# VectorE takes the wide sums and products that GpSimd did in the mixers of a two-layer hybrid decoder

## The chip, the core and the metric

The kernel runs on one core of a Trainium2 chip. The metric is the device time of one execution, in microseconds (us). The times shown are the median of three runs; the profile is one further execution of the same program, with its own time. Engines are named as the profile names them: PE is TensorE (matmuls), DVE is VectorE (elementwise work), ACT is ScalarE (copies and functions), POOL is GpSimd, SP is SyncE, which here only issues DMAs.

## What is computed

Two decoder layers over 1024 positions of 1024 channels, all in float32. Each layer is a mixer and a squared-ReLU MLP of width 4096, each with a norm ahead of it and a norm behind it. Layer 0 mixes with a gated linear recurrence (HGRN2, 4 heads) and with retention (4 heads), layer 1 with a matrix memory (mLSTM, 4 heads).

```python
def reference(x, norm_g, ...):
    for l in range(DEPTH):                       # DEPTH = 2
        g = norm_g[l]
        h = rmsnorm(x, g[0])
        if l % 2 == 0:
            y = even_mixer(h, ev_w_in[e], lower_bounds[l], ev_hg_norm_g[e], ev_ret_norm_g[e], ev_w_out[e])
        else:
            y = odd_mixer(h, od_w_in[o], od_conv_w[o], od_conv_b[o], od_gate_b[o], od_ml_norm_g[o], od_w_out[o])
        x = x + rmsnorm(y, g[1])
        h = rmsnorm(x, g[2])
        x = x + rmsnorm(sq_relu_mlp(h, mlp_w1[l], mlp_w2[l]), g[3])
    return x
...
def sq_relu_mlp(h, w1, w2):
    return jnp.square(jax.nn.relu(h @ w1)) @ w2
```

The mixers are projections (`h @ w_in`), per-head work on chunks (gates, RoPE, scans over a state, a norm per head, a gate with silu or sigmoid) and an output projection (`y @ w_out`).

## The kernel before

**Matmuls.** Every large product is done in seven block products in place of eight (Strassen-Winograd), so both operands need sums and differences of blocks ahead of the matmuls. Every operand is also split in two parts of lower precision, hi and lo, and each product is three matmuls (hi·hi, hi·lo, lo·hi). A weight block therefore goes through these steps: a DMA lands it in one of four buffers `raw` (`pump`, line 140); the Winograd sums are made in place in `raw` and in one spare tile `ws` (`operands`, lines 174 to 207, the instruction itself on lines 188 and 190); ScalarE copies each operand to `hi` (line 160); VectorE subtracts to get `lo` (line 161). `hi` and `lo` have three buffers each, so up to three units are prepared ahead of TensorE.

**Who makes the sums.** `operands` takes an engine. The MLP (`mlp_plan`) passes VectorE; the mixers use the default, GpSimd (`pair_preps` and `group_preps`), so their sums run on line 190. Four more places in the mixers use GpSimd for wide operations: two of the four sums in `right_sums` (line 413, the activations' Winograd sums), the product in `silu_gate` (line 613), the last sum in `rope` (line 729), and the residual sum in `post_finish` (line 509), except in `mixer_last`, which passes VectorE. Besides, GpSimd does short chains of operations that are one column wide (1 element in each of 128 partitions): `rsq` (lines 127 and 128), lines 498, 516, 784, 786, 979, 980 and 982. Each head's scan squares a chunk on ScalarE, sends the sum of squares through such a chain on GpSimd and multiplies the output by the result on VectorE (lines 722, 788, 984). GpSimd also issues the DMAs that write the hidden activations of the MLP (line 1148).

**Order.** A planner sets the order of the instructions on each engine ahead of time, from its own estimate of the durations; each engine then runs its list in that order and waits where an operand is not there yet. Among the instructions that are ready, the planner takes the one that comes first in the program. `tc.high_priority(offset=-100)` moves the instructions in its block some 100 places back in that preference: in the kernel before, the split (lines 160 and 161) and VectorE's weight sums (line 188) are moved back in this way, GpSimd's weight sums (line 190) are not.

**Stages.** In the trace, layer 0's mixer takes about 0 to 680 us, its MLP 680 to 1500, layer 1's mixer 1500 to 2000, its MLP 2000 to 2704. Each mixer does its 1024 positions in two halves; between them lies the output projection with `post_finish` (`mixer_out`).

Of the kernel before, what the change touches and what calls it, by code (L numbers as in the profile page):

```python
# [7 lines left out]
F32 = mybir.dt.float32  # L8
# [4 lines left out]
ALU = mybir.AluOpType  # L13
# [56 lines left out]
def hybrid_kernel(ctx, tc, x, norm_g, pv_d, cs_d, mk_d, dec_d, cos_d, sin_d, wg_d, gb_d, w_ev, w_od, w_mlp, out):  # L70
    nc = tc.nc
# [5 lines left out]
    XT = ("z0", "z1", "x2", "x3")  # L77
# [78 lines left out]

    def split_w(dst, src):
        hi, lo = dst
        with tc.high_priority(offset=-100):
            nc.scalar.copy(out=hi, in_=src)  # L160
            nc.vector.tensor_tensor(out=lo, in0=src, in1=hi.bitcast(F32), op=ALU.subtract)  # L161

    def new_pair(i):
        return (wp.tile([P, 1024], F32R, tag="hi", name=f"whi{i}"),
# [6 lines left out]
        free_raw()  # L171
        return hl

    def operands(wide, eng):

        if wide:
            a11, a21, a22, a12 = (take_raw() for _ in range(4))
            t = wp.tile([P, 1024], F32, tag="ws", bufs=1, name="ws")
        else:
            r1, r2 = take_raw(), take_raw()  # L180
            a11, a12 = r1[:, 0:512], r1[:, 512:1024]
            a21, a22 = r2[:, 0:512], r2[:, 512:1024]
            t = wp.tile([P, 1024], F32, tag="ws", bufs=1, name="ws")[:, 0:512]

        def op(o, x0, x1, f):
            if eng is nc.vector:
                with tc.high_priority(offset=-100):
                    eng.tensor_tensor(out=o, in0=x0, in1=x1, op=f)  # L188
            else:
                eng.tensor_tensor(out=o, in0=x0, in1=x1, op=f)  # L190

        op(t, a21, a22, ALU.add)
        yield a11
        yield t
        op(a21, a11, a21, ALU.subtract)
        op(a11, t, a11, ALU.subtract)
        yield a11
        yield a12
        op(a12, a12, a11, ALU.subtract)
        if wide:  # L200
            free_raw()
        yield a21
        if wide:
            free_raw()
        yield a12
        yield a22
        free_raw(2)

    def rest_operands():

        r1, r2 = take_raw(), take_raw()
        a11, a12 = r1[:, 0:512], r1[:, 512:1024]
        a21, a22 = r2[:, 0:512], r2[:, 512:1024]
        t = wp.tile([P, 1024], F32, tag="ws", bufs=1, name="ws")[:, 0:512]

        def op(o, x0, x1, f):
            with tc.high_priority(offset=-100):
                nc.vector.tensor_tensor(out=o, in0=x0, in1=x1, op=f)

        op(t, a21, a22, ALU.add)  # L220
        op(a21, a11, a21, ALU.subtract)
        op(a11, t, a11, ALU.subtract)
        yield a11
        yield t
        yield a21
        op(a12, a12, a11, ALU.subtract)
        yield a12
        yield a22
        free_raw(2)

    def pair_preps(n, eng=nc.gpsimd, begun=0):
        gen = {}
        todo = [(p, o, o == 0, o == last) for p in range(n) for last in [4 if p < begun else 6] for o in range(last + 1)]

        def prep(j):
            def run(i):
                hl = new_pair(i)
                for e, (p, o, first, last) in enumerate(todo[2 * j:2 * j + 2]):
                    if first:
                        gen[p] = rest_operands() if p < begun else operands(False, eng)  # L240
                    c = slice(e * 512, (e + 1) * 512)
                    split_w((hl[0][:, c], hl[1][:, c]), next(gen[p]))
                    if last:
                        next(gen[p], None)
                return hl
            return run
        return [prep(j) for j in range((len(todo) + 1) // 2)]

    def group_preps(eng=nc.gpsimd):
        gen = []  # L250

        def prep(o):
            def run(i):
                hl = new_pair(i)
                if o == 0:
                    gen.append(operands(True, eng))
                split_w(hl, next(gen[0]))
                if o == 6:
                    next(gen[0], None)
                return hl  # L260
            return run
        return [prep(o) for o in range(7)]

    BEGUN = 3

    def mlp_plan():
        units = [std_prep] * BEGUN + pair_preps(16, nc.vector, BEGUN)
        for _ in range(7):
            units += group_preps(nc.vector)
        return units + [std_prep] * 8  # L270

    plan = []
# [48 lines left out]
    def add(o, x0, x1):  # L321
        nc.vector.tensor_tensor(out=o, in0=x0, in1=x1, op=ALU.add)  # L322
# [85 lines left out]

    def right_sums(stage):
        b11, b12, t1, t2, b21, t3, b22, t4 = (z[:, c] for z in stage for c in (L, R))  # L410
        for o, x0, x1, eng in ((t1, b12, b11, nc.vector), (t2, b22, t1, nc.vector),
                               (t3, b22, b12, nc.gpsimd), (t4, b21, t2, nc.gpsimd)):
            eng.tensor_tensor(out=o, in0=x0, in1=x1, op=ALU.subtract)  # L413

    def right_split(stage, k, p11, tiles):
        def split(dst, src):
# [76 lines left out]
        junk = sm.tile([P, 512], BF16, tag="junk", bufs=1, name="junk")  # L493
        nc.scalar.activation(out=junk, in_=y, func=AF.Square, accum_out=ss[t][:, n:n + 1])

    def post_finish(s, half, t, parts, ss, grow, tags=("z0", "z1"), eng=nc.gpsimd):
        tot = sm.tile([P, 1], F32, tag="tot", name=f"tot{s}_{half}_{t}")
        nc.gpsimd.tensor_tensor(out=tot, in0=ss[t][:, 0:1], in1=ss[t][:, 1:2], op=ALU.add)
        rs = sm.tile([P, 1], F32, tag="rs", name=f"rs{s}_{half}_{t}")
# [4 lines left out]
        for n in range(2):  # L504
            c = slice(n * 512, (n + 1) * 512)
            tmp = rg.tile([P, 512], F32, tag="tmp", bufs=2, name="ptmp")
            nc.vector.scalar_tensor_tensor(out=tmp, in0=parts[n], scalar=rs, in1=grow[:, c],
                                           op0=ALU.mult, op1=ALU.mult)
            eng.tensor_tensor(out=xt[:, c], in0=xt[:, c], in1=tmp, op=ALU.add)
            if s < 3:  # L510
                junk = sm.tile([P, 512], BF16, tag="junk", bufs=1, name="junk")
                nc.scalar.activation(out=junk, in_=xt[:, c], func=AF.Square, accum_out=s2[:, n:n + 1])
# [26 lines left out]
    def mixer_last(s, yT):  # L539

        grow = load_grow(s)
# [9 lines left out]
        xn = []  # L551
        for t in range(NT):
            post_sq(p1[t], t, 1, ss)
            xt = post_finish(s, 1, t, [y0[t], p1[t]], ss, grow, XT, nc.vector)
            parts = [kt.tile([P, HALF], F32, tag="kt", name=f"xk{s}_{t}_{n}") for n in range(2)]
            for n in range(2):
                nc.scalar.activation(out=parts[n], in_=xt[:, n * 512:(n + 1) * 512], func=AF.Copy, scale=rstd[1, t])
            xn.append(parts)
# [50 lines left out]
    def silu_gate(c, nm):  # L609
        for j in range(2):  # L610
            tmp = rg.tile([P, 2, 256], F32, tag="tmp", bufs=2, name=nm + f"sg{j}")
            nc.scalar.activation(out=tmp, in_=c[j], func=AF.Sigmoid)
            nc.gpsimd.tensor_tensor(out=c[j], in0=c[j], in1=tmp, op=ALU.mult)

    def scan_states(home, nm):

# [107 lines left out]
    def rope(c, cos, sin):  # L724
# [1 line left out]
        nc.vector.tensor_tensor(out=tmp[64:128], in0=c[0:64], in1=sin[0:64], op=ALU.mult)  # L726
        nc.vector.tensor_tensor(out=tmp[0:64], in0=c[64:128], in1=sin[64:128], op=ALU.mult)
        nc.vector.tensor_tensor(out=c, in0=c, in1=cos, op=ALU.mult)
        nc.gpsimd.tensor_tensor(out=c, in0=c, in1=tmp, op=ALU.add)

    def rt_keys(half, h, hT, cos, sin):
        nm = f"rt{half}_{h}"
# [691 lines left out]
```

## Time and profile before

| | before |
|---|---|
| median of 3 runs | 2698.22 us (2695.55 to 2700.66) |
| the profiled execution: its time | 2706.18 us |
| its span, from the first to the last instruction | 2704.4 us |
| PE busy | 2467.0 us (91%) |
| DVE busy | 1980.1 us (73%) |
| ACT busy | 1204.1 us (45%) |
| POOL busy | 780.4 us (29%) |

Busy time counts every stretch in which an engine has an instruction in work, once, however long that instruction takes; time in which the engine waits for a semaphore is idle, and the profile names what ended it.

### The profile page before, as it was taken

The numbers are of one execution on the slowest core, as the hardware profiler recorded it, in microseconds if no ns is written. First come the engines' busy times: TensorE is split into PE (matmuls) and PEld (weight loads), VectorE is DVE, ScalarE is ACT, GpSimd is POOL, SyncE is SP. The second block draws the span as 40 slices with busy tenths as digits, with TensorE's granted clock in tenths as the row PEclk, the third lists the DMA queues.
The fourth block names the chain that finished last, engine by engine and source line by source line (L and its number), as shares of the span: only waits on it lengthen the run. The fifth ranks groups of instructions, "written<-read, shape, count | busy, mean of one in ns | idle before, by whom it ended". The sixth has DMA issues, their size and how long they took to land. (4 is left out here: it accounts for less than half of the span.)

```text
span 2704.4 us, 41553 instructions
## 1 busy us (share of the span) xinstructions
PE 2467.0 (91%) x16432; PEld 2239.8 (83%) x16432; DVE 1980.1 (73%) x2574; ACT 1204.1 (45%) x2080; POOL 780.4 (29%) x895
## 2 busy tenths in 40 slices
PE   6989998898897999999998688988988999999997
PEld 6888888898885888899997588888866888899996
DVE  7898868889748666657774798789757666766774
ACT  5444454444445443443344544554455434443332
POOL 5665437665311111100001345376320111100000
PEclk8999999999998999999999899999999999999999
DMA  3222323122232434453453222232233433554353
GB/s 137 69 73 78 110 86 118 63 79 71 94 140 102 168 144 156 171 198 126 160 172 125 103 87 79 100 133 69 96 134 108 169 145 140 210 178 136 129 174 140
DMA packets 92836, 335.91 MB, mean 124 GB/s; under 512 B 10848, under 2 KB 10976, under 8 KB 92640
## 3 DMA queue, kind: packets, MB, share of 16 engines
q1 hardware_dynamic: 75744, 272.42, 29.6%
q0 software_dynamic: 16896, 60.83, 5.9%
q8 instruction: 129, 2.11, 0.3%
q14 instruction: 67, 0.55, 0.1%
HBM read 255.61 MB, written 77.59 MB: 123 GB/s over the span
## 5 line engine op out<-in xcount | busy, mean ns | idle before, releaser
L160 ACT CAST whi<-raw 128x512 fp32r<-128x512 f32 (+1 forms) x590 | 469.6, 812 | 684.4 <-PE p_0x L1168 72.4
L161 DVE TENSOR_TENSOR wlo<-raw,whi 128x512 fp32r<-128x512 f32 (+1 forms) x590 | 583.7, 1005 | 192.3 <-ACT whi L160 174.1
L1279 POOL TENSOR_TENSOR rs<-pm 128x1 f32<-128x1 f32 (+1 forms) x7 | 2.2, 321 | 635.2 <-ACT junk L1263 635.2
L190 POOL TENSOR_TENSOR raw<-raw,raw 128x1024 f32<-128x1024 f32 (+1 forms) x64 | 151.1, 2361 | 83.3 <-DVE wlo L161 41.5
L160 ACT CAST whi<-ws 128x512 fp32r<-128x512 f32 (+1 forms) x90 | 70.4, 782 | 101.4 <-POOL ws L190 34.7
L190 POOL TENSOR_TENSOR raw<-ws,raw 128x512 f32<-128x512 f32 (+1 forms) x44 | 88.6, 2014 | 62.1 <-DVE wlo L161 42.1
L161 DVE TENSOR_TENSOR wlo<-ws,whi 128x512 fp32r<-128x512 f32 (+1 forms) x90 | 96.8, 1075 | 9.0 <-ACT whi L160 9.0
L190 POOL TENSOR_TENSOR ws<-raw,raw 128x1024 f32<-128x1024 f32 x20 | 51.1, 2555 | 39.3 <-DMA raw<-in_w_ev_dram 30.8
L322 DVE TENSOR_TENSOR ya<-p_0x,ya 128x1024 f32<-128x1024 f32 x26 | 31.8, 1222 | 34.9 <-PE p_0x L1169 34.9
L188 DVE TENSOR_TENSOR raw<-raw,raw 128x1024 f32<-128x1024 f32 (+1 forms) x54 | 52.0, 963 | 0.5
L413 POOL TENSOR_TENSOR xb_a<-xb_a,xb_a 128x256 f32<-128x256 f32 x32 | 34.2, 1079 | 56.4 <-ACT xb_a L479 50.4
L190 POOL TENSOR_TENSOR ws<-raw 128x512 f32<-128x512 f32 x24 | 36.3, 1513 | 46.8 <-DMA raw<-in_w_od_dram 25.5
L190 POOL TENSOR_TENSOR raw<-raw 128x512 f32<-128x512 f32 x24 | 36.7, 1528 | 32.4 <-DVE wlo L161 32.4
L1166 PE MATMUL p_0v<-whi,h_5R1h 128*128 128x256 f32 x128 | 36.6, 286 | 3.1 <-ACT h_5R1h L1019 3.1
L1166 PE MATMUL p_0v<-whi,h_1R0h 128*128 128x256 f32 x128 | 35.9, 281 | 2.9 <-ACT m_15h L340 2.9
L1168 PE MATMUL p_0v<-whi,h_5R1l 128*128 128x256 f32 x128 | 36.7, 287 | 1.8 <-DVE h_5R1l L1020 1.8
L1166 PE MATMUL p_0x<-whi,h_4L1h 128*128 128x256 f32 x128 | 35.8, 280 | 1.1 <-ACT whi L160 1.1
L1166 PE MATMUL p_0x<-whi,h_2L0h 128*128 128x256 f32 x128 | 36.0, 281 | 0.6 <-ACT ya L1173 0.6
L1169 PE MATMUL p_0v<-wlo,h_5R1h 128*128 128x256 f32 x128 | 36.4, 285 | 0.0
L1168 PE MATMUL p_0z<-whi,h_3L4l 128*128 128x256 f32 x128 | 35.9, 280 | 0.3 <-DVE h_3L4l L1020 0.3
L1168 PE MATMUL p_0v<-whi,h_1R0l 128*128 128x256 f32 x128 | 35.8, 280 | 0.0
L1169 PE MATMUL p_0x<-wlo,h_2L0h 128*128 128x256 f32 x128 | 35.8, 279 | 0.0
(5385 smaller groups left out, 10111.4 us busy)
## 6 DMA issues: line engine op xcount, KB each, us to landing
raw<-in_w_mlp_dram SPq DMA_DIRECT2D x142, 512.0 KB, 3.7
h<-hid SPq DMA_DIRECT2D x112, 512.0 KB, 4.3
raw<-in_w_ev_dram SPq DMA_DIRECT2D x104, 512.0 KB, 3.3
raw<-in_w_od_dram SPq DMA_DIRECT2D x64, 512.0 KB, 3.3
xs<-xr SPq DMA_DIRECT2D x24, 512.0 KB, 2.9
xr<-xs SPq DMA_DIRECT2D x24, 512.0 KB, 5.2
xn<-in_x_dram SPq DMA_DIRECT2D x8, 512.0 KB, 3.8
xr<-in_x_dram SPq DMA_DIRECT2D x8, 512.0 KB, 5.3
```

Source lines behind the costliest of these rows:

```text
L160: nc.scalar.copy(out=hi, in_=src)
L161: nc.vector.tensor_tensor(out=lo, in0=src, in1=hi.bitcast(F32), op=ALU.subtract)
L188: eng.tensor_tensor(out=o, in0=x0, in1=x1, op=f)
L190: eng.tensor_tensor(out=o, in0=x0, in1=x1, op=f)
L322: nc.vector.tensor_tensor(out=o, in0=x0, in1=x1, op=ALU.add)
L413: eng.tensor_tensor(out=o, in0=x0, in1=x1, op=ALU.subtract)
L1166: nc.tensor.matmul(a, h[:, c], hi[:, w], start=first and k == 0 and t % 2 == 0, stop=False, skip_group_check=True)
L1168: nc.tensor.matmul(a, l[:, c], hi[:, w], start=False, stop=False, skip_group_check=True)
L1169: nc.tensor.matmul(a, h[:, c], lo[:, w], start=False, stop=k == 3, skip_group_check=True)
L1279: nc.gpsimd.tensor_tensor(out=rs[:, z], in0=ss[half][:, 0, z], in1=ss[half][:, 1, z], op=ALU.add)
```

## The change

All wide operations of GpSimd in the mixers are given to VectorE: the weight sums of `operands`, the two sums of `right_sums`, the product of `silu_gate`, the last sum of `rope` and the residual sum of `post_finish`. GpSimd keeps the chains that are one column wide, a memset and the DMAs of the MLP. In the same edit, the weight splits and VectorE's weight sums lose their offset: they stand in the planner's preference at their place in the program, in the MLP too.

```diff
     def split_w(dst, src):
         hi, lo = dst
-        with tc.high_priority(offset=-100):
-            nc.scalar.copy(out=hi, in_=src)
-            nc.vector.tensor_tensor(out=lo, in0=src, in1=hi.bitcast(F32), op=ALU.subtract)
+        nc.scalar.copy(out=hi, in_=src)
+        nc.vector.tensor_tensor(out=lo, in0=src, in1=hi.bitcast(F32), op=ALU.subtract)
...
-    def operands(wide, eng):
+    def operands(wide):
...
         def op(o, x0, x1, f):
-            if eng is nc.vector:
-                with tc.high_priority(offset=-100):
-                    eng.tensor_tensor(out=o, in0=x0, in1=x1, op=f)
-            else:
-                eng.tensor_tensor(out=o, in0=x0, in1=x1, op=f)
+            nc.vector.tensor_tensor(out=o, in0=x0, in1=x1, op=f)
...
     def rest_operands():
         def op(o, x0, x1, f):
-            with tc.high_priority(offset=-100):
-                nc.vector.tensor_tensor(out=o, in0=x0, in1=x1, op=f)
+            nc.vector.tensor_tensor(out=o, in0=x0, in1=x1, op=f)
...
     def right_sums(stage):
         b11, b12, t1, t2, b21, t3, b22, t4 = (z[:, c] for z in stage for c in (L, R))
-        for o, x0, x1, eng in ((t1, b12, b11, nc.vector), (t2, b22, t1, nc.vector),
-                               (t3, b22, b12, nc.gpsimd), (t4, b21, t2, nc.gpsimd)):
-            eng.tensor_tensor(out=o, in0=x0, in1=x1, op=ALU.subtract)
+        for o, x0, x1 in ((t1, b12, b11), (t2, b22, t1), (t3, b22, b12), (t4, b21, t2)):
+            nc.vector.tensor_tensor(out=o, in0=x0, in1=x1, op=ALU.subtract)
...
     def post_finish(...)
-            eng.tensor_tensor(out=xt[:, c], in0=xt[:, c], in1=tmp, op=ALU.add)
+            add(xt[:, c], xt[:, c], tmp)
...
     def silu_gate(c, nm):
-            nc.gpsimd.tensor_tensor(out=c[j], in0=c[j], in1=tmp, op=ALU.mult)
+            nc.vector.tensor_tensor(out=c[j], in0=c[j], in1=tmp, op=ALU.mult)
...
     def rope(c, cos, sin):
-        nc.gpsimd.tensor_tensor(out=c, in0=c, in1=tmp, op=ALU.add)
+        nc.vector.tensor_tensor(out=c, in0=c, in1=tmp, op=ALU.add)
```

## Rows read from the trace of the kernel before

**Rows 1.** The page: engines' busy time, share of the span, instructions.

```profile
PE 2467.0 (91%) x16432; PEld 2239.8 (83%) x16432; DVE 1980.1 (73%) x2574; ACT 1204.1 (45%) x2080; POOL 780.4 (29%) x895
```

**Rows 2.** Stretches: from:to, length, busy us of each engine (instructions), granted clock, DMA.

```profile
60.00:300.00 240.00, 217.14 (x1770) 209.85 (x1769) 211.87 (x291) 100.78 (x198) 146.30 (x120) 0.97 0.23 77
...
420.00:680.00 260.00, 229.44 (x1842) 223.26 (x1840) 228.02 (x294) 112.41 (x221) 168.27 (x143) 0.95 0.25 84
680.00:1500.00 820.00, 775.07 (x4829) 689.34 (x4830) 543.77 (x667) 358.78 (x549) 96.75 (x150) 0.98 0.42 146
1500.00:1850.00 350.00, 297.40 (x2070) 272.61 (x2068) 287.27 (x415) 176.96 (x359) 176.19 (x196) 0.93 0.28 96
1850.00:2000.00 150.00, 138.18 (x905) 126.02 (x906) 108.91 (x170) 71.19 (x134) 53.97 (x78) 0.98 0.29 99
```

**Rows 3.** Groups on POOL by shape, whole run: busy us, mean ns | idle before.

```profile
L190 POOL TENSOR_TENSOR raw<-raw,raw 128x1024 f32<-128x1024 f32 x40 | 110.2, 2754 | 81.9 <-DVE wlo L161 41.5 <-issue 39.6
...
L190 POOL TENSOR_TENSOR raw<-raw,raw 128x512 f32<-128x512 f32 x24 | 41.0, 1707 | 1.3
...
L413 POOL TENSOR_TENSOR xb_a<-xb_a,xb_a 128x256 f32<-128x256 f32 x32 | 34.2, 1079 | 56.4 <-ACT xb_a L479 50.4 <-DVE xb_a L413 4.8 <-DVE lbt L592 1.0
L509 POOL TENSOR_TENSOR xr<-xr,ptmp 128x512 f32<-128x512 f32 x16 | 25.8, 1630 | 8.7 <-DVE ptmp L507 6.9 <-PE o L393 0.9 <-issue 0.9
...
L729 POOL TENSOR_TENSOR rt_1kq<-rt_1kq,rtmp 128x512 f32<-128x512 f32 x4 | 9.3, 2325 | 11.9 <-DVE rt_1kq L728 11.9
```

**Rows 4.** Groups on DVE by shape, 1000 to 1350 us (the MLP, no sums on POOL).

```profile
L161 DVE TENSOR_TENSOR wlo<-raw,whi 128x1024 fp32r<-128x1024 f32 x31 | 37.8, 1218 | 8.6 <-ACT whi L160 8.6
L161 DVE TENSOR_TENSOR wlo<-raw,whi 128x512 fp32r<-128x512 f32 x41 | 26.7, 686 | 24.8 <-ACT whi L160 18.6 <-PE m_15y L1099 3.1 <-PE m_13y L1099 3.1
```

**Rows 5.** The same groups of line 161 on DVE, whole run.

```profile
L161 DVE TENSOR_TENSOR wlo<-raw,whi 128x1024 fp32r<-128x1024 f32 x266 | 340.9, 1284 | 76.5 <-ACT whi L160 75.2 <-PE tp L464 1.0
L161 DVE TENSOR_TENSOR wlo<-raw,whi 128x512 fp32r<-128x512 f32 x324 | 243.0, 776 | 115.8 <-ACT whi L160 98.9 <-PE tp L1037 6.8 <-PE m_15y L1099 3.1
L161 DVE TENSOR_TENSOR wlo<-ws,whi 128x512 fp32r<-128x512 f32 x56 | 48.8, 872 | 5.7 <-ACT whi L160 5.7
```

**Rows 6.** Whole run, DVE busy of line 676, then of line 677 (128x256 each).

```profile
0.00:2704.00 2704.00, 47.50 (x56) 0.97 0.36 124
...
0.00:2704.00 2704.00, 53.81 (x56) 0.97 0.36 124
```

**Rows 7.** Whole run, DVE busy of line 726 (64x512).

```profile
0.00:2704.00 2704.00, 28.15 (x16) 0.97 0.36 124
```

**Rows 8.** Instructions in order of time on DVE, then POOL: start us, us, engine, line.

```profile
631.64 1.23 DVE L161 TENSOR_TENSOR wlo<-raw,whi 128x1024 fp32r<-128x1024 f32 x1 [0.32 <-ACT whi L160]
632.78 0.42 DVE L322 TENSOR_TENSOR rt_2kq<-rt_2py,rt_2kq 128x256 f32<-128x256 f32 x1
633.24 2.42 DVE L726 TENSOR_TENSOR rtmp<-rt_2kq,rot 64x512 f32<-64x512 f32 x1
635.67 2.78 DVE L727 TENSOR_TENSOR rtmp<-rt_2kq,rot 64x512 f32<-64x512 f32 x1
...
632.13 2.98 POOL L190 TENSOR_TENSOR ws<-raw,raw 128x1024 f32<-128x1024 f32 x1 [5.36 <-DMA raw<-in_w_ev_dram]
635.19 2.72 POOL L190 TENSOR_TENSOR raw<-raw,raw 128x1024 f32<-128x1024 f32 x1
```

**Rows 9.** Waits of DVE, whole run: who <- whom, total us, times, longest.

```profile
DVE gate L788 <- POOL rt_3rs L786: 14.7, 8, 2.8
...
DVE gate L788 <- POOL rt_2rs L786: 3.3, 7, 0.8
```

**Rows 10.** Waits of PE, whole run.

```profile
PE hg_1s L648 <- DVE hg_1ca L667: 6.3, 2, 4.3
...
PE mv_3x L319 <- DVE wlo L161: 4.9, 2, 2.9
```

**Rows 11.** Waits of POOL, whole run.

```profile
POOL ws L190 <- DMA raw<-in_w_ev_dram: 45.3, 20, 5.9
```

More of the change, by code (lines that the diff above doesn't have):

```diff
@@ L229, in rest_operands, with pair_preps @@
         free_raw(2)
-    def pair_preps(n, eng=nc.gpsimd, begun=0):
+    def pair_preps(n, begun=0):
         gen = {}
@@ L239, in run @@
                     if first:
-                        gen[p] = rest_operands() if p < begun else operands(False, eng)
+                        gen[p] = rest_operands() if p < begun else operands(False)
                     c = slice(e * 512, (e + 1) * 512)
@@ L247, in pair_preps, with group_preps @@
         return [prep(j) for j in range((len(todo) + 1) // 2)]
-    def group_preps(eng=nc.gpsimd):
+    def group_preps():
         gen = []
@@ L255, in run @@
                 if o == 0:
-                    gen.append(operands(True, eng))
+                    gen.append(operands(True))
                 split_w(hl, next(gen[0]))
@@ L266, in mlp_plan @@
     def mlp_plan():
-        units = [std_prep] * BEGUN + pair_preps(16, nc.vector, BEGUN)
+        units = [std_prep] * BEGUN + pair_preps(16, BEGUN)
         for _ in range(7):
-            units += group_preps(nc.vector)
+            units += group_preps()
         return units + [std_prep] * 8
@@ L494, in post_sq, with post_finish @@
         nc.scalar.activation(out=junk, in_=y, func=AF.Square, accum_out=ss[t][:, n:n + 1])
-    def post_finish(s, half, t, parts, ss, grow, tags=("z0", "z1"), eng=nc.gpsimd):
+    def post_finish(s, half, t, parts, ss, grow, tags=("z0", "z1")):
         tot = sm.tile([P, 1], F32, tag="tot", name=f"tot{s}_{half}_{t}")
@@ L553, in mixer_last @@
             post_sq(p1[t], t, 1, ss)
-            xt = post_finish(s, 1, t, [y0[t], p1[t]], ss, grow, XT, nc.vector)
+            xt = post_finish(s, 1, t, [y0[t], p1[t]], ss, grow, XT)
             parts = [kt.tile([P, HALF], F32, tag="kt", name=f"xk{s}_{t}_{n}") for n in range(2)]
```

## The prediction

> **What bounds the kernel now.** I read the page's busy times first, then the stretches by stage, then the groups by shape on VectorE and GpSimd, then the waits. TensorE is busy 91% of the span [rows 1], so no more than some 240 us can be had at all. By stage the picture splits. In the MLP (680 to 1500 us) TensorE is busy 775 of 820 us and VectorE 544: TensorE bounds it, and VectorE has room. In the mixers VectorE is nearly as full as TensorE: 212 against 217 of 240 us, 228 against 229 of 260, 287 against 297 of 350, 109 against 138 of 150 [rows 2]. In these four stretches TensorE is idle for 22.9, 30.6, 52.6 and 11.8 us, 118 us together. Its longer waits there are for VectorE: the recurrence's chain (line 648 behind line 667) and the split of the weights (line 319 behind line 161) [rows 10]. So the mixers are bound by two engines at once, and what VectorE gains or loses there passes on to TensorE in part.
>
> VectorE's time there isn't all work. The split of a 128x512 weight block takes 686 ns in the MLP, where GpSimd makes no sums [rows 4], and 776 ns over the whole run [rows 5]; no shape has changed. Rows in order of time show why. At 632.78 a sum on VectorE that reads PSUM takes its 0.42 us although GpSimd has been at a 2.98 us sum since 632.13. The next one, a product of two SBUF tensors (64x512, as many columns as the 686 ns split), takes 2.42 us and ends at 635.66, half a microsecond behind GpSimd's sum (635.11). The one behind that takes 2.78 us and ends at 638.45, as far behind GpSimd's second sum (635.19 and 2.72 us) [rows 8]. VectorE's operations on two SBUF tensors are held while GpSimd makes a wide sum. GpSimd is held by VectorE too: its 128x512 sums take 1707 ns in this group, its 128x1024 ones 2754 [rows 3].
>
> **What moves, and its cost on VectorE.** 264 instructions: weight sums, 80 of 128x1024 (three groups, of 40, 20 and 20) and 96 of 128x512 (four groups of 24); 32 of line 413, 16 of line 509, 16 of line 729 (four groups of 4) [rows 3]; and 24 of line 613, by the code six calls of two in each half. VectorE's prices, free of GpSimd, are 1218 ns for 128x1024 and 686 ns for 128x512 [rows 4], 0.42 us for 128x256 (the sum at 632.78, which reads PSUM, the nearest row for line 413) [rows 8]. That is 80 x 1.218 = 97.4, 152 x 0.686 = 104.3 and 32 x 0.42 = 13.4, together 215 us. Neighbours overlap by 0.09 us (631.64 + 1.23 against 632.78 [rows 8]), so 264 x 0.09 = 24 us come off: **+191 us** for VectorE.
>
> **What goes from VectorE.** The hold-ups. Line 161: 266 x (1284 - 1218) = 17.6, 324 x (776 - 686) = 29.2, 56 x (872 - 686) = 10.4 us [rows 4, 5]. Lines 676 and 677: 47.5 + 53.8 less 112 x 0.42 = 54.3 us [rows 6]. Line 726: 28.15 less 16 x 0.686 = 17.2 us [rows 7]. These five groups make 129 us, the lower end. Not counted are line 727 (line 726's twin [rows 8]), the convolution, the scans, the activations' splits and the rest, some 200 instructions by the code; an estimate at the loss of lines 676, 677 and 726 (71.5 us in 128 instructions, 0.56 us each) is 112 us, so the upper end is 240. I take 200, as the mixers' remaining operations on two SBUF tensors are of the same kind and lie in the same stretches. **-200 us**. VectorE's load in the mixers thus stays as it is: -9 us, with ends of +62 and -49.
>
> One rule of the Trainium skill speaks against the change. "Perfetto Trace Analysis", section "Optimizing Scalar/DVE Operations", says that where VectorE is saturated, giving some work to ScalarE or even GpSimd may make sense, and adds that VectorE and GpSimd share an SBUF read port, so that between these two it might not help. By the first half alone the change would put 191 us on an engine that is 88% busy (that case is priced as a rival below); the rows on the split and on the two rope products side with the second half.
>
> **What else gets shorter.** VectorE waits idle for GpSimd's one-column chains at the end of each scan step: twelve rows between 14.7 and 3.3 us, 84 us in all (the first and the last are shown) [rows 9]. A chain queues behind wide sums of 1.5 to 2.8 us [rows 3]. With these gone only its own short operations are left, and VectorE, which waits in order with the splits and sums behind the waiting product, goes on sooner. How much of the 84 us is queueing the trace doesn't say: between nothing and two thirds; I take a third, **-28 us**. The weight sums themselves get shorter, three in a row from 3 x 2.75 to 3 x 1.22 us, so `lo` comes sooner to TensorE's waits on line 161 [rows 3, 4, 10].
>
> **The offset that is dropped.** Splits and VectorE's sums now stand at their place in the program and not 100 places later. In the mixers this brings weights earlier and the recurrence's chain later; both feed TensorE. In the MLP TensorE idles 45 of 820 us and VectorE has 276 us of room [rows 2], which hides a shift of either sign; without that cover a split late by its own length costs 1.2 us a unit. I take 0, between -10 and +15 for both MLPs.
>
> **The sum.** VectorE gets -9 - 28 = -37 us in the mixers. TensorE is idle 118 us there and waits partly for DMAs, ScalarE and its own chain, so I let two thirds arrive: -25 us. The profiled execution took 2706.18 us (2704.4 us of span and 1.8 around it), 8 us above the median of the three runs. 2706.18 - 25 = 2681; against the median, 2698.2 - 25 = **2673 us**.
>
> **Rivals.**
>
> *The hold-ups weigh more.* If VectorE is the true bound and the uncounted lines reach the upper end, it gets -49 - 28 - 10 (more of the chains) = -87 us, and TensorE's pieces at half its granted clock behind such waits (0.93 and 0.95 in two of the stretches [rows 2]) go too. Nearly all arrives: about 2620 us. For it: three of the four stretches have VectorE within 11 us of TensorE's busy time. Against: TensorE's waits for VectorE that head the list are 4.3 and 2.9 us long at most [rows 10]; its idle time is spread thin.
>
> *Hidden.* VectorE's load is unchanged, and the shorter chains are waited for by nobody but VectorE. Then the time stays within 5 us: 2698.
>
> *Slower: VectorE waits for weights with the mixer behind it.* Today GpSimd waits for weight DMAs ahead of a sum, 45.3 us in 20 waits in the even mixer alone [rows 11]; there it delays nothing but sums. VectorE runs its list in order, so a sum that stands too early, as it may without the offset, holds the recurrence's products and the scans' updates behind it. The point from which it decides: when such waits on VectorE in the mixers exceed the 37 us that it gains. If the even mixer's 45.3 us come over whole, with as much in the odd one, VectorE is at +91 - 37 = +54 us, and two thirds of that arrive: 2734 us. For it: waits of 2.3 us each that don't depend on who makes the sum. Against: an engine that is 88% busy reaches its sums later than GpSimd, which is 60% busy, does (212 and 146 of 240 us [rows 2]), so more weights will have landed.
>
> *The change doesn't do what it should: the hold-ups aren't GpSimd's.* Then VectorE pays 191 us and gets nothing back: it would need 212 + 50 of 240 us in the first stretch and 228 + 55 of 260 in the second, and the mixers stretch by about 100 us: 2800. The rows at 632 to 638 us speak against it: the ends follow GpSimd's ends, and the sum that reads PSUM isn't held.
>
> **How the numbers follow.** Forecast, 2673 (between 2655 and 2690): 0.46. Hold-ups weigh more, near 2620 to 2650: 0.12. Hidden: 0.12. Slower, near 2710 to 2745: 0.27. Hold-ups not GpSimd's: 0.03. The range of 8 in 10 takes in the forecast, the hidden case, the near part of the larger gain and most of the slower one: 2630 to 2732. What a measurement of this kernel can tell from no change is about 0.2%, 5.4 us. Faster by more than that: 0.58; within: 0.12; slower: 0.30.
>
> **What would show it.** Right: line 161 at 686 and 1218 ns in the mixers too, lines 676 and 677 at 0.42 us throughout, line 726 at 0.69; GpSimd at some 290 us busy; VectorE's total within 50 us of 1980; its waits for lines 128, 786 and 982 down to about 56 us; TensorE's idle time in the four stretches below 118 us. Wrong: VectorE's waits for weight DMAs in the mixers above 37 us, or long waits of TensorE for the recurrence's chain (lines 667 to 677), which the dropped offset would put later, or an MLP longer by more than 15 us.

## The result, and the profile after

The changed kernel takes 2605.47 us (median of four runs, 2603.22 to 2608.68) against 2699.44 us (four runs, 2695.55 to 2700.76) before: a ratio of 0.9655, with a 95% interval of [0.9638, 0.9672], 94 us less. The direction was forecast; the size lies outside the range, 25 us below its lower end.

The profiled execution took 2604.44 us, of which 2602.6 us are its span, 101.8 us less than before (more than the 94 us, since the profiled execution of the kernel before took 6.7 us more than the median). The page, busy time of each engine as in [rows 1]:

```profile
PE 2441.2 (94%) x16432; PEld 2218.7 (85%) x16432; DVE 1923.3 (74%) x2838; ACT 1203.0 (46%) x2080; POOL 330.4 (13%) x631
```

Look at DVE: 264 instructions more and 56.8 us *less* busy. TensorE executes the same 16432 instructions and is busy 25.8 us less; its mean granted clock rose from 0.966 to 0.980 of 2.4 GHz. So 76 us of the 101.8 are idle time of TensorE that is gone. The other 26 us fit the clock: by the two traces' records of the granted clock, 125 us of TensorE's busy time lay at the lower of its two levels, 1.2 GHz, before and 68 us do now, and the same work at 2.4 GHz takes half of the 57 us between them.

Where it went can be read from one instruction that closes a stage, the MLP's first matmul, in order of time (start us, us, engine, line). In the kernel before:

```profile
802.47 0.39 PE L1097 MATMUL m_0x<-bT_R0h,whi 128*128 128x512 f32 x1
```

And in the changed one:

```profile
753.73 0.39 PE L1090 MATMUL m_0x<-bT_R0h,whi 128*128 128x512 f32 x1
```

Layer 0's mixer, up to there, is 48.7 us shorter. (It lasts to 802 us in the kernel before, not to 680 as the stages ahead of the prediction have it. The stretch from 680 to 1500 us, read there as the MLP, begins with 122 us of mixer, and the four stretches called the mixers are 1000 of their 1304 us.) Layer 1's takes 1447.1 to 1901.3 us instead of 1499.5 to 2001.7, 48.0 us less. The two MLPs share the other 5 us.

By stretch, in the columns of [rows 2] (length, then busy us of PE, PEld, DVE, ACT, POOL, granted clock, DMA), for the same four parts of the mixers and the MLP between them:

```profile
57.00:267.00 210.00, 204.96 (x1740) 201.06 (x1739) 195.87 (x342) 100.11 (x197) 29.31 (x56) 0.99 0.25 84
389.00:616.00 227.00, 215.34 (x1799) 210.47 (x1798) 206.25 (x346) 113.06 (x223) 37.83 (x71) 0.98 0.28 96
754.00:1447.00 693.00, 657.94 (x4153) 587.45 (x4151) 475.33 (x588) 301.05 (x447) 55.46 (x84) 0.98 0.44 153
1447.00:1753.00 306.00, 284.61 (x2063) 261.87 (x2063) 262.57 (x470) 173.55 (x351) 74.17 (x131) 0.98 0.32 110
1753.00:1901.00 148.00, 138.87 (x919) 126.70 (x920) 110.94 (x196) 74.47 (x144) 28.19 (x63) 0.99 0.29 100
```

With nearly as many matmuls (1740 for 1770, 1799 for 1842, 2063 for 2070, 919 for 905), the four stretches are 210 + 227 + 306 + 148 us long instead of 240 + 260 + 350 + 150, and TensorE is idle for 5.0, 11.7, 21.4 and 9.1 us: 47 us in place of 118. In the first of them it is now busy 205 of 210 us.

VectorE's groups by shape, whole run, as in [rows 4, 5] (lines have moved: 161 is now 160, the sums of 188 and 190 are 185, 676 and 677 are 669 and 670, 726 is 719):

```profile
L160 DVE TENSOR_TENSOR wlo<-raw,whi 128x1024 fp32r<-128x1024 f32 x266 | 323.4, 1220 | 68.4 <-ACT whi L159 67.1 <-PE tp L457 1.3
L160 DVE TENSOR_TENSOR wlo<-raw,whi 128x512 fp32r<-128x512 f32 x324 | 216.1, 688 | 120.7 <-ACT whi L159 112.4 <-PE tp L1030 7.9
L160 DVE TENSOR_TENSOR wlo<-ws,whi 128x512 fp32r<-128x512 f32 x56 | 38.5, 687 | 0.0
L185 DVE TENSOR_TENSOR raw<-raw,raw 128x1024 f32<-128x1024 f32 x68 | 83.0, 1221 | 0.1
L670 DVE TENSOR_TENSOR hg_1ca<-hg_1ca,hg_1ca 128x256 f32<-128x256 f32 x14 | 6.0, 426 | 0.0
```

The split takes 688 ns over the *whole* run, where it took 776, and 1220 where it took 1284; the third group went from 872 to 687. The moved sums take 1221 ns. The recurrence's product is at 0.43 us, where lines 676 and 677 had averaged 0.85 and 0.96 [rows 6]. The rope's two products, 2.42 and 2.78 us in [rows 8], in order of time:

```profile
222.73 0.69 DVE L719 TENSOR_TENSOR rtmp<-rt_2kq,rot 64x512 f32<-64x512 f32 x1
223.43 0.69 DVE L720 TENSOR_TENSOR rtmp<-rt_2kq,rot 64x512 f32<-64x512 f32 x1
```

VectorE's waits (who <- whom: us in total, times, longest), the two that answer to [rows 9], and the one for a weight of the even mixer:

```profile
DVE gate L781 <- POOL rt_3rs L779: 11.5, 7, 2.1
DVE gate L781 <- POOL rt_2rs L779: 3.7, 3, 2.1
...
DVE ws L185 <- DMA raw<-in_w_ev_dram: 3.8, 4, 1.7
```

All waits of that kind for the three scan chains (the twelve rows of the prediction) together went from 84.1 to 56.4 us; the waits for the norms' chains, which run on GpSimd too, stayed at about 45 us (46.2 before, 45.2 after). VectorE's waits for weights in the mixers are 3.8 us in the even and 1.7 in the odd one.

### The profile page after: what moved, and what is told of

It is laid out like the page before. It is cut to its first block, busy times and chain, and to the rows that moved or that the text cites. A ratio compares the mean times of both kernels' runs of the same rounds, so it can differ in the third digit from the quotient of the medians.

```text
span 2602.6 us, 41370 instructions
## 1 busy us (share of the span) xinstructions
PE 2441.2 (94%) x16432; PEld 2218.7 (85%) x16432; DVE 1923.3 (74%) x2838; ACT 1203.0 (46%) x2080; POOL 330.4 (13%) x631
## 5 line engine op out<-in xcount | busy, mean ns | idle before, releaser
L160 DVE TENSOR_TENSOR wlo<-raw,whi 128x512 fp32r<-128x512 f32 (+1 forms) x590 | 539.4, 928 | 189.2 <-ACT whi L159 179.5
L185 DVE TENSOR_TENSOR raw<-raw,raw 128x1024 f32<-128x1024 f32 (+1 forms) x118 | 117.4, 995 | 0.5
L185 DVE TENSOR_TENSOR raw<-ws,raw 128x512 f32<-128x512 f32 (+1 forms) x84 | 76.0, 904 | 0.9
L185 DVE TENSOR_TENSOR ws<-raw,raw 128x1024 f32<-128x1024 f32 x34 | 41.6, 1223 | 21.2 <-DMA raw<-in_w_mlp_dram 17.3
L185 DVE TENSOR_TENSOR ws<-raw 128x512 f32<-128x512 f32 x50 | 34.5, 690 | 17.2 <-DMA raw<-in_w_mlp_dram 15.4
L1159 PE MATMUL p_0v<-whi,h_1R0h 128*128 128x256 f32 x128 | 35.9, 281 | 2.8 <-ACT m_15h L334 2.8
L1159 PE MATMUL p_0v<-whi,h_5R1h 128*128 128x256 f32 x128 | 35.9, 281 | 2.2 <-ACT h_5R1h L1012 2.2
L1161 PE MATMUL p_0v<-whi,h_5R1l 128*128 128x256 f32 x128 | 35.9, 281 | 1.8 <-DVE h_5R1l L1013 1.8
L1159 PE MATMUL p_0x<-whi,h_2L0h 128*128 128x256 f32 x128 | 35.9, 281 | 0.5 <-ACT ya L1166 0.5
L1159 PE MATMUL p_0x<-whi,h_0L3h 128*128 128x256 f32 x128 | 35.8, 280 | 0.5 <-ACT whi L159 0.5
L1161 PE MATMUL p_0z<-whi,h_3L4l 128*128 128x256 f32 x128 | 35.9, 280 | 0.1
L1162 PE MATMUL p_0x<-wlo,h_0L3h 128*128 128x256 f32 x128 | 35.8, 280 | 0.0
L1162 PE MATMUL p_0x<-wlo,h_6L2h 128*128 128x256 f32 x128 | 35.8, 280 | 0.0
L1162 PE MATMUL p_0v<-wlo,h_1R0h 128*128 128x256 f32 x128 | 35.8, 280 | 0.0
L1162 PE MATMUL p_0x<-wlo,h_4L1h 128*128 128x256 f32 x128 | 35.8, 280 | 0.0
```

What stands on the lines that cost most here:

```text
L1159: nc.tensor.matmul(a, h[:, c], hi[:, w], start=first and k == 0 and t % 2 == 0, stop=False, skip_group_check=True)
L1161: nc.tensor.matmul(a, l[:, c], hi[:, w], start=False, stop=False, skip_group_check=True)
L1162: nc.tensor.matmul(a, h[:, c], lo[:, w], start=False, stop=k == 3, skip_group_check=True)
```

## The experiments

Two theories stood at the outset. *Hold-ups*: GpSimd's wide sums held VectorE's operations on two SBUF tensors, and taking them away gives the time back. *Order and queueing*: the dropped offset, or the chains of GpSimd that no longer stand behind wide sums, give it. A third question came with the size: what a microsecond of VectorE's time is worth in the mixers.

The runs were made in groups, each beside runs of its own of the kernel before, whose median lay between 2699.4 and 2703.3 us. A ratio compares within a group. A difference of two times from different groups is good to some 5 to 7 us. The planner orders each of these kernels anew, and what another order alone is worth no run shows apart from the offset's.

**Which half of the edit.** The kernel before with the offset dropped and nothing moved:

```diff
-        with tc.high_priority(offset=-100):
-            nc.scalar.copy(out=hi, in_=src)
-            nc.vector.tensor_tensor(out=lo, in0=src, in1=hi.bitcast(F32), op=ALU.subtract)
+        nc.scalar.copy(out=hi, in_=src)
+        nc.vector.tensor_tensor(out=lo, in0=src, in1=hi.bitcast(F32), op=ALU.subtract)
```

> The kernel before with the offset alone dropped; GpSimd keeps its sums. Theory A (VectorE's time in the mixers decides: hold-ups by GpSimd against the price of the moved sums): the hold-ups stay, line 161's 128x512 split stays near 776 ns on average, and the time stays at 2690 to 2710 us. Theory B (weights that are prepared earlier decide, and the dropped offset brings them): at least half of the 94 us comes from here, 2650 us or less.

Measured: 2699.96 us, 0.9994 [0.9982, 1.0007]. The split's row (whole run) stays where it was:

```profile
L160 DVE TENSOR_TENSOR wlo<-raw,whi 128x512 fp32r<-128x512 f32 x324 | 247.5, 785 | 121.5 <-ACT whi L159 113.9 <-PE tp L1031 6.8
```

And the reverse, the kernel before with all wide operations moved and the offsets kept:

```diff
             if eng is nc.vector:
                 with tc.high_priority(offset=-100):
                     eng.tensor_tensor(out=o, in0=x0, in1=x1, op=f)
             else:
-                eng.tensor_tensor(out=o, in0=x0, in1=x1, op=f)
+                nc.vector.tensor_tensor(out=o, in0=x0, in1=x1, op=f)
```

> The move alone: all wide operations of GpSimd in the mixers go to VectorE, the offsets stay where they were (splits and the MLP's sums 100 places back, the moved sums at their place). Theory A: 2595 to 2620 us, all of the gain. Theory B: 2650 us or more.

Measured: 2600.54 us, 0.9625 [0.9605, 0.9644], VectorE 1920.4 us busy. The offset alone shows no effect; the move alone gives all of the gain. The changed kernel run once more gave 2603.66 us, 0.9643 [0.963, 0.9657], between its two expectations; its interval and that of the move alone overlap.

> The changed kernel once more, against the kernel before on the same chip, so that the small differences of the move alone (0.9625) and of the version with more on ScalarE (0.9616) can be told from it. If these two are faster than the changed kernel: its ratio stays at 0.965 or above. If not: 0.961 to 0.964.

**Which of the moved operations.** The changed kernel with the mixers' 176 weight sums left on GpSimd; the other 88 moved:

```diff
-            nc.vector.tensor_tensor(out=o, in0=x0, in1=x1, op=f)
+            eng.tensor_tensor(out=o, in0=x0, in1=x1, op=f)
...
-    def pair_preps(n, begun=0):
+    def pair_preps(n, eng=nc.gpsimd, begun=0):
```

> The changed kernel, but the weight sums of the mixers (176 of the 264 moved instructions, 364 of 491 us on GpSimd) stay on GpSimd; the other 88 are on VectorE. Theory A: the gain goes with GpSimd's wide time that is taken away, 127 of 491 us, 26% of 94 us: 2675 us (2660 to 2685). Theory C (the shorter chain of weight sums ahead of TensorE is the gain): 2690 us or more, since the weights are as late as before.

Measured: 2672.31 us, 0.9887 [0.9872, 0.9901]. This is what the first expectation said. So the 88 others are worth 27 us and the weight sums 67. And the changed kernel without these 176 sums altogether:

```diff
-            nc.vector.tensor_tensor(out=o, in0=x0, in1=x1, op=f)
+            if more:
+                nc.vector.tensor_tensor(out=o, in0=x0, in1=x1, op=f)
```

> The changed kernel without the weight sums of the mixers: the 176 instructions are left out and the splits take the plain blocks, so that the mixers' projections are not computed; 80 x 1.14 + 96 x 0.60 = 149 us less for VectorE there, everything else stays. If VectorE still bounds the mixers of the changed kernel, at the share with which the 148 us of the spare sums arrived (0.72 to 0.75): 2490 to 2510 us. If TensorE has become the bound (it is busy 205 of 210 us and 215 of 227 us in the two even stretches): only what TensorE idles in the mixers can come, 2550 us or more.

Measured: 2533.65 us, 0.9373 [0.9358, 0.9388], between the two expectations. The page of the one without the sums:

```profile
PE 2409.7 (95%) x16432; PEld 2195.9 (87%) x16432; DVE 1784.5 (71%) x2662; ACT 1203.3 (48%) x2080; POOL 289.6 (11%) x631
```

And of the one with the sums on GpSimd (2672.31 us):

```profile
PE 2461.1 (92%) x16432; PEld 2236.2 (84%) x16432; DVE 1973.3 (74%) x2662; ACT 1202.4 (45%) x2080; POOL 673.0 (25%) x807
```

These two rows are the clearest of the case: VectorE executes the same 2662 instructions in both, and 176 sums *on GpSimd* make it 189 us busier. On VectorE the same sums cost it 139 us (1923.3 - 1784.5). In time, they cost 139 us on GpSimd (2672 - 2534), 0.73 of what they held, and 72 on VectorE (2605.5 - 2533.7), 0.52 of what they lasted there.

**Is it the reading, or the queue?** The changed kernel with spare work on GpSimd beside the mixers' weights, which writes a tile that nothing reads: once 256 sums of two SBUF tensors, once 512 memsets behind 176 one-column reads that tie them to the same places, once 256 copies.

```diff
+    def extra(hi, lo, n):
+        for b in range(0, n, 512):
+            nc.gpsimd.tensor_tensor(out=scr, in0=hi[:, b:b + 512].bitcast(F32), in1=lo[:, b:b + 512].bitcast(F32), op=ALU.add)
...
+                    if more and o < 4:
+                        extra(hl[0][:, c], hl[1][:, c], 512)
```

> The changed kernel with 256 more sums on GpSimd in the mixers, 128x512 each, which read two SBUF tensors (the hi and lo of a finished split) and write a spare tile that nothing reads: some 370 us of GpSimd, with no one waiting for them. Theory A: VectorE is held about half as long as GpSimd works (248 of 491 us before), 185 us, and all of it arrives: 2750 to 2800 us. Theory C: nobody waits for these sums, 2605 to 2625 us.

Measured: 2808.14 us, 1.0387 [1.037, 1.0404]. The page:

```profile
PE 2513.9 (90%) x16432; PEld 2272.3 (81%) x16432; DVE 2116.7 (75%) x2838; ACT 1203.2 (43%) x2080; POOL 783.7 (28%) x887
```

The spare sums' group on GpSimd (busy us, mean ns | idle before):

```profile
L177 POOL TENSOR_TENSOR scr<-whi,wlo 128x512 f32<-128x512 f32 x256 | 447.3, 1747 | 381.0 <-DVE wlo L160 338.3 <-DVE hg_0ts L681 11.3 <-DVE hg_2ts L681 8.5
```

VectorE, with no instruction more, is 193 us busier, and the time is 203 us longer, a little above the first expectation. Its waits for the three scan chains are 57.2 us in total, where the changed kernel has 56.4, so it isn't these chains that cost here. But "with no one waiting for them" doesn't hold: ScalarE may write the next `hi` only when the spare sum that reads the old one is done. Waits of ScalarE's splits, in this run:

```profile
ACT whi L159 <- DVE raw L191: 128.5, 49, 7.4
ACT whi L159 <- POOL scr L177: 80.1, 37, 5.6
ACT whi L159 <- DVE ws L191: 32.2, 11, 7.3
```

Now the memsets:

```diff
+        nc.gpsimd.tensor_tensor(out=scr[:, 0:1], in0=hi[:, 0:1].bitcast(F32), in1=lo[:, 0:1].bitcast(F32), op=ALU.add)
+        for _ in range(n // 256):
+            nc.gpsimd.memset(scr, 0.0)
```

> The changed kernel with GpSimd kept as long, but without reading: in place of each spare sum of 128x512 a one-column sum that ties it to the split, and two memsets of 128x512 (525 ns each before), 512 memsets, some 270 us. GpSimd's one-column chains queue behind them, VectorE's operations are to be held by nothing but the one-column reads. Theory A1 (the hold-ups are the cost): 2605 to 2635 us. Theory A2 (the chains that queue on GpSimd are the cost): VectorE's waits for lines 128, 779 and 975 go up again by 28 us or more, and the time is 2640 us or more.

Measured: 2629.86 us, 0.9725 [0.971, 0.9741]. The page:

```profile
PE 2445.7 (93%) x16432; PEld 2222.5 (85%) x16432; DVE 1925.5 (73%) x2838; ACT 1206.0 (46%) x2080; POOL 705.8 (27%) x1319
```

The groups of the memsets and of the reads that tie them:

```profile
L178 POOL MEMSET scr<- 128x512 f32 x512 | 272.8, 533 | 27.3
L176 POOL TENSOR_TENSOR scr<-whi,wlo 128x1 f32<-128x1 f32 x176 | 122.8, 698 | 288.2 <-DVE wlo L160 249.5 <-DVE ml_0tot L925 11.7 <-DVE hg_2ts L682 9.8
```

GpSimd is nearly as busy as with the sums (706 against 784 us), and VectorE's busy time doesn't move (1925.5 for 1923.3). So busy time of GpSimd as such doesn't hold VectorE; its wide reads of SBUF do. The Trainium skill, "SBUF — State Buffer", section "Who interferes with whom", says just that: a VectorE instruction with two SBUF inputs contends with a GpSimd instruction that reads SBUF, and not with one that only writes it; +193 against +2 us agree. The queue has a price of its own: VectorE's waits for the three scan chains rise by 17.2 us (56.4 to 73.6), those for all one-column chains, the norms' with them, by 24.4 (101.6 to 126.0), and the time by 24.4. Last, the copies, which read one tensor:

```diff
+            nc.gpsimd.tensor_copy(out=scr, in_=lo[:, b:b + 512].bitcast(F32))
```

> The changed kernel with 256 spare copies of 128x512 on GpSimd in the mixers, SBUF to SBUF, one input in place of the sums' two. If a read of SBUF by GpSimd is enough to hold VectorE: VectorE's busy time rises by 80 us or more over 1923 us and the time is 2700 us or more. If only a second input holds it: 2605 to 2640 us, as with the memsets.

Measured: 2651.55 us, 0.9806 [0.9785, 0.9827]. The page:

```profile
PE 2455.0 (93%) x16432; PEld 2228.6 (84%) x16432; DVE 1974.7 (75%) x2838; ACT 1204.3 (45%) x2080; POOL 637.2 (24%) x887
```

The copies' group:

```profile
L177 POOL COPY scr<-wlo 128x512 f32<-128x512 f32 x256 | 299.9, 1171 | 367.8 <-DVE wlo L160 349.1 <-DVE ml_1rr L980 3.6 <-DVE mv_2va L946 3.6
```

The time lies between the expectations: copies hold VectorE too, 51 us for 300 us of GpSimd (0.17 of it), where the sums held it 193 for 447 (0.43).

**What a microsecond of VectorE is worth.** The same spare sums on VectorE, in the mixers beside the weights (`nc.vector` for `nc.gpsimd` in `extra`): 256 of them, then 512, then 128; and 240 in the MLP.

> The changed kernel with the same 256 spare sums of 128x512 in the mixers, on VectorE: 256 x 0.60 = 154 us more for VectorE, which nobody waits for. If VectorE bounds the mixers, all of it arrives: 2740 to 2770 us. If two thirds arrive, as the prediction had it: 2708 us.

> The changed kernel with 512 spare 128x512 sums on VectorE in the mixers (twice those of the kernel with 256; they read the finished hi and lo and write a tile that nothing reads). The first 256 added 148 us to VectorE's busy time and 111 us to the time, 0.75 of it; the mixers' own weight sums added 139 and 72, 0.52 of it. If what arrives grows as VectorE fills, the second 256 (some 148 us more) cost at least as much as they last: 2840 to 2870 us. If two thirds arrive at any load, they cost 77 to 111 us: 2793 to 2827 us.

> The changed kernel with 128 spare 128x512 sums on VectorE in the mixers, half of the kernel with 256, some 74 us of VectorE's time. If what arrives grows as VectorE fills, between 0.52 and 0.75 of them: 2643 to 2654 us. If the share is that of the 256 from the start, 0.75: 2660 us. This is also the point at which VectorE's total is that of the kernel in which the mixers' weight sums stay on GpSimd (2672 us, some 1975 us busy): if holding VectorE costs no more than loading it, this kernel, with some 20 us more load, comes out at 2665 us or above.

> The changed kernel with 240 spare sums of 128x512 on VectorE behind the splits of the MLP, 144 us there. TensorE bounds the MLP and VectorE has room: 2600 to 2615 us. If load on VectorE costs time wherever it lies: 2700 us or more.

Measured: 2716.29 us, 1.0039 [1.0019, 1.0058]; 2851.66 us, 1.0545 [1.0522, 1.0568]; 2658.01 us, 0.983 [0.981, 0.985]; and in the MLP 2613.58 us, 0.967 [0.965, 0.9691]. The page with 256 spare sums in the mixers:

```profile
PE 2478.7 (91%) x16432; PEld 2243.3 (83%) x16432; DVE 2071.3 (76%) x3094; ACT 1209.9 (45%) x2080; POOL 355.6 (13%) x631
```

With 512:

```profile
PE 2543.4 (89%) x16432; PEld 2296.2 (80%) x16432; DVE 2225.3 (78%) x3350; ACT 1213.2 (43%) x2080; POOL 381.5 (13%) x631
```

With 128:

```profile
PE 2458.3 (93%) x16432; PEld 2230.5 (84%) x16432; DVE 1994.7 (75%) x2966; ACT 1205.6 (45%) x2080; POOL 347.0 (13%) x631
```

With 240 in the MLP (this load costs 8 us of time):

```profile
PE 2431.1 (93%) x16432; PEld 2208.5 (85%) x16432; DVE 2062.6 (79%) x3078; ACT 1204.5 (46%) x2080; POOL 333.3 (13%) x631
```

Put in order of VectorE's busy time, with the kernel without sums as the start, load beside the weights has this price:

| VectorE busy | time | step | of it arrives |
|---|---|---|---|
| 1784.5 (no sums) | 2533.65 | | |
| 1923.3 (changed kernel) | 2605.47 | +138.8: +71.8 | 0.52 |
| 1994.7 (128 spare) | 2658.01 | +71.4: +52.5 | 0.74 |
| 2071.3 (256 spare) | 2716.29 | +76.6: +58.3 | 0.76 |
| 2225.3 (512 spare) | 2851.66 | +154.0: +135.4 | 0.88 |

A share of one of the two short steps is good to some 0.1, of a long one to some 0.05. So 0.74 and 0.76 can't be told apart: 128 spare sums came out near the 2660 us of a constant share and not at the 2643 to 2654 of one that grows, and 256 between their two expectations. What differs is the first step, 0.52, and the last, 0.88. Two causes fit that, and no run separates them: VectorE fills, or the spare sums cost more than their time on VectorE. The first step is made of the sums themselves; spare sums also keep `hi` from being overwritten, as on GpSimd. Waits of ScalarE's splits with 256 of them, then with 512:

```profile
ACT whi L159 <- DVE scr L177: 90.3, 51, 6.5
ACT whi L159 <- DVE raw L191: 32.4, 21, 4.9
ACT whi L159 <- DVE ws L191: 10.8, 11, 2.3
...
ACT whi L159 <- DVE scr L177: 143.2, 67, 6.9
```

The kernel with 128 spare sums also answers whether held time costs more than planned load: its VectorE is busy 21 us longer than with the weight sums on GpSimd (1994.7 against 1973.3), and it takes 14 us less (2658.0 against 2672.3). It does, together with what the sums' longer durations on GpSimd cost by themselves.

In the MLP, 139 us more of VectorE cost 8 us, not told apart from nothing: there is room.

Is it the same wherever VectorE's time is taken? 240 products by one, 128x512, put into the chains of the mixers in place of beside the weights:

```diff
+    def again(c, n=1):
+        o = one if len(c.shape) == 2 else one.rearrange("p (a b) -> p a b", a=2)
+        for _ in range(n):
+            nc.vector.tensor_tensor(out=c, in0=c, in1=o, op=ALU.mult)
...
             nc.vector.tensor_tensor(out=s_end, in0=s_end, in1=f_end, op=ALU.mult)
+            again(ks)
+            again(qp)
```

> The changed kernel with 240 spare products by one, 128x512, on VectorE, put in place of the weights into the chains of the mixers: two behind each level of the recurrence (112), two behind each rope (32), two behind each gate's product (48), one behind each step of the convolution (48). Some 145 us of VectorE's time, as much as the 256 spare sums beside the weights, which cost 111 us. If it matters where VectorE's time is taken, and holding costs more than load because it also strikes the chains, nearly all arrives or more: 2740 to 2770 us. If time of VectorE costs the same wherever it is taken, 0.75 of it: 2705 to 2725 us.

Measured: 2756.99 us, 1.0201 [1.0182, 1.022]. The page:

```profile
PE 2494.4 (91%) x16432; PEld 2258.9 (82%) x16432; DVE 2063.9 (75%) x3079; ACT 1205.1 (44%) x2080; POOL 334.2 (12%) x631
```

TensorE's waits, the longest in total:

```profile
PE hg_3s L650 <- DVE hg_3ca L179: 26.4, 8, 5.8
```

It matters: 140.6 us more of VectorE cost 151.5 us, 1.08 of it, against 0.75 for as much beside the weights. TensorE now stands behind the recurrence (26.4 us in eight waits for one head, over both halves, where the largest such total of the changed kernel, behind line 671, is 5.3).

**Is there more to be had?** 56 further operations of VectorE (copies, scalings and a bias) given to ScalarE, once on top of the changed kernel, once on top of the kernel that keeps the offsets:

```diff
-            nc.vector.tensor_copy(out=y0[t], in_=p0[t])
+            nc.scalar.copy(out=y0[t], in_=p0[t])
...
-                nc.vector.tensor_scalar_mul(xt, xt, r)
+                nc.scalar.activation(out=xt, in_=xt, func=AF.Copy, scale=r)
```

> The changed kernel with 56 more instructions of VectorE given to ScalarE (46% busy): the copies of the output projection out of PSUM (16), the scaling ahead of the first norm (8), two of the recurrence's gate operations (16) and the convolution's first tap (16); some 33 us of VectorE in the mixers. If VectorE bounds the mixers and ScalarE hides the work: 2565 to 2585 us. If the longer steps on ScalarE lie in the chain instead: 2600 us or more.

> The move alone, with the offsets kept, and the 56 instructions given to ScalarE besides. If the two small differences (the move alone against the changed kernel, the changed kernel with more on ScalarE against itself) add up: 2590 to 2600 us. If TensorE bounds the even mixers by now: 2598 to 2606 us, as each of them alone.

Measured: 2601.42 us, 0.9616 [0.9596, 0.9636], and 2612.29 us, 0.9662 [0.9647, 0.9678]. VectorE is 28 and 25 us less busy, ScalarE 37 and 35 us busier. The first time is 4 us below the changed kernel's, within the noise, as its second expectation had it. The second is 12 us above the move alone, clear of both intervals and outside both expectations: a miss. That TensorE leaves nothing to win can't be the reason, since the kernel without the sums is 72 us faster. That the longer steps on ScalarE lie in the chain fits, but no run tests it, and the 12 us stay open.

## Why the prediction was right or wrong

**Right.** The mechanism, its prices, and what is not in it.

- *Prices on VectorE.* 1218 and 686 ns were used, 1221 and 688 measured; lines 676 and 677 came to 0.42 us, line 726 to 0.69. By these prices the 176 weight sums cost VectorE 147 us; the kernel without them shows 139. The moved work at +191 us needs little correction.
- *Whose hold-ups they were.* GpSimd's sums: the pair of pages with 2662 instructions shows it by addition, the memsets against the spare sums show that it is their reading. The rival "hold-ups aren't GpSimd's" falls.
- *Chains.* Waits down to "about 56 us": 56.4. The third that was taken was a choice between nothing and two thirds, so this hit is luck.
- *The offset at 0.* 0.9994 by itself.
- *The slower rival.* It needed over 37 us of VectorE's waits for weights in the mixers; there are 5.5. That fits the argument against it (a full engine reaches its sums late, when the weights have landed).
- Of what the Trainium skill says on giving VectorE's work to GpSimd ("Perfetto Trace Analysis", section "Optimizing Scalar/DVE Operations"), the second half, which the prediction gave the greater weight, decided: here taking work back from GpSimd made VectorE less busy.

**Wrong: the term of the hold-ups.** 200 us were taken out of 129 to 240. VectorE's busy time fell by 56.8 us with 191 us added: 191 + 57 = 248 us were held, above the upper end. The counted lines were right (129 us said, 126 measured). The rest was guessed short: the five counted groups left 71 of the 200 us for it, and it came to some 120, near the 112 that the prediction had worked out for its upper end. In it are line 727 with 12.6 us, the convolution's sums (line 887) with 17.9 and the activations' split (line 418) with 14.1. Some of it isn't of the kind that the prediction named: lines 634, 636 and 884, which read one wide tensor each, went from 32.7 to 16.4 us in their 32 instructions. And not all of that kind was held: line 728, which reads two SBUF tensors right behind lines 726 and 727, took 10.95 us in 16 instructions before and 10.98 after.

VectorE's net was thus -57, not -9, and with the chains -57 - 28 = -85 us in place of -37. That is the sum of the rival "the hold-ups weigh more" (-87), which stood at 0.12 and 2620 us.

**Wrong: two thirds arrive, of everything.** With the right terms the rule would still have given 0.67 x 85 = 57 us, 2641; 94 came. The runs put two prices in its place:

- Load on VectorE in this region is worth 0.74 (1923 to 1995 us): 57 x 0.74 = 42 us. The share was close here by luck: the step below this region has 0.52, the one above 2071 us 0.88.
- Waits for one-column chains are worth at least their length: with the memsets VectorE's waits for all of them rose by 24.4 us and so did the time, 1 each; set against the 17.2 us of the scan chains alone, it is 1.42 each. The 27.7 us that went are thus 28 to 39 us. The prediction took them, as all else, at two thirds.

Together that is 70 to 81 of 94 us; 13 to 24 us are left over. The rule gives one price to all of VectorE's time, but held time costs more than planned load. Two pairs of runs show that: 0.73 against 0.52 for the weight sums (on GpSimd and on VectorE), 1.05 against 0.75 for 256 spare sums (203 us of time for 193 us held, 111 for 148 us of load). Whole runs split the 94 us without any price: 27 us for the 88 others, and for the weight sums the 139 us that they cost on GpSimd less the 72 on VectorE.

Why held time costs more, the runs show only in part. *The sums come sooner*: ScalarE's splits waited 101.6 us for GpSimd's sums before and wait 67.8 for VectorE's now, 34 us less; the prediction named this and gave it no price. Before, then after:

```profile
ACT whi L160 <- POOL raw L190: 66.9, 44, 3.4
ACT whi L160 <- POOL ws L190: 34.7, 14, 4.9
...
ACT whi L159 <- DVE raw L185: 48.1, 29, 4.1
ACT whi L159 <- DVE ws L185: 19.7, 9, 4.8
```

With 256 spare sums on GpSimd these waits for the weight sums are 160.7 us, with the same spare sums on VectorE 43.2, while the waits for the spare sums themselves are nearly the same (80.1 and 90.3). *Holding strikes chains*: time taken in the chains costs 1.08, beside the weights 0.75. In the run with spare sums on GpSimd, VectorE's time in lines 669 to 671 of the changed kernel rose from 61.9 to 94.4 us, the rope's four from 43.9 to 61.5 and the convolution's from 35.9 to 50.4: 65 of the 193 us fell on chains. But a third on chains at 1.08 and the rest at 0.75 make 0.86, not 1.05, so place alone doesn't explain it. No run gives the late weights a price of their own.

*TensorE's clock.* The forecast left it out; the larger rival had it. The 26 us that TensorE's busy time lost are part of the gain, not beside it. Over the runs the clock goes with TensorE's idle time (0.985 at 120 us idle in the kernel without sums, 0.949 at 310 with 512 spare sums); that the shorter waits raised it is argued from that, and no run tests it alone.

*A reading of the waits.* The prediction has TensorE's longer waits in the four stretches as waits for VectorE. The longest single ones there were for ScalarE, 8.8 us (line 857 behind 417) and 4.5 (line 648 behind 160); they enter no term.

## What to carry to other kernels

Before giving a second engine work, look for rows of the first whose shape hasn't changed and whose duration has: two pages with the same instruction count (2662) and 189 us between them say more than any busy share, and the loss can exceed what the work would cost at home (139). Price held time, planned load and waits for a chain each by itself: here a microsecond held cost 0.73 and 1.05, one of planned load 0.52 to 0.88 in the mixers and next to nothing in the MLP, and one of waiting for a chain 1 to 1.4. Where only part of the held operations is counted, read the rest from the trace line by line, or take the size that an estimate gives it; here the estimate of 112 us was at hand, 71 were taken, and some 120 came.

## What the runs showed of the hardware that was not expected

- A GpSimd memset of 128x512 takes 533 ns, and 512 of them cost VectorE 2 us of busy time; 256 copies that read one tensor cost it 51 us, 256 sums that read two 193 us. By the Trainium skill ("SBUF — State Buffer", section "Who interferes with whom") a GpSimd instruction that reads SBUF contends, without a distinction between one input and two; here the share of GpSimd's time that VectorE is held differs, 0.17 and 0.43.
- GpSimd is held in turn. Its one-column power of line 128 took 94.07 us in 145 instructions before and 102.08 after, although GpSimd lost all its wide work, and 90.00 in the kernel without the weight sums:

```profile
0.00:2704.00 2704.00, 94.07 (x145) 0.97 0.36 124
...
0.00:2603.00 2603.00, 102.08 (x145) 0.98 0.37 129
...
0.00:2530.00 2530.00, 90.00 (x145) 0.98 0.39 133
```

  With the same 631 instructions GpSimd is busy 289.6 us without the mixers' weight sums on VectorE, 330.4 with them (290 were forecast), and 347.0, 355.6 and 381.5 with 128, 256 and 512 spare ones beside the weights. 240 more in the chains or in the MLP hardly change it (334.2 and 333.3); why the place matters, no run shows.
